# Branch B by halves of the queries, the third group's Q and K by residue, and merge sums on VectorE: one hybrid attention block on one core

## The chip, the cores and the metric

The kernel runs on 1 core of one Trainium2 chip. The metric is the device time of one execution in microseconds. Three runs of the kernel before are shown; its profile is one more execution.

## The reference

One decoder layer in float32, 2,048 tokens of width 1,024, batch 1. Token mixing: a normalised and modulated `h` goes through one input projection into two branches.

Branch A has 12 heads of 64 in three groups of 4, with (window, dilation) of (128, 1), (512, 4) and (2048, 16). A query at position t sees t, t-d, t-2d, ..., within the window, with a linear bias. The three groups' outputs are merged for each of 4 head slots with weights from their softmax denominators. Branch B has 4 heads of causal attention over all earlier tokens, with a forgetting bias:

```
qa, ka, va, qb, kb, vb, fz, gza, gzb = split(h @ w_in)
ya = dilated_mixture(qa, ka, va) @ w_up_a
yb = forgetting_attention(qb, kb, vb, fz, b_forget) @ w_up_b
x  = x + g1 * ((sigmoid(gza) * ya + sigmoid(gzb) * yb) @ w_out)
```

A gated feed-forward part and a last norm follow; the change doesn't touch them.

## The kernel before

All matrices are split into a high and a low part and multiplied in three products (`mm3`, L99) or, for scores, two. Stages in the order of the text: input projections, written to DRAM scratch; the two attention branches; the merge ("up"); the output projection; the feed-forward part. `build` (L1168) hands the whole trunk to a tile framework that places the instructions on the engines' queues from the order of the text and a planned timeline, allots buffers by tag and sets all waits. So the order of the text sets priorities and isn't kept to the letter.

Q and K (`qk_block`, L399). A projected block of 128 columns (two heads) by 512 tokens is evicted by `put` (L405) and stored to `qk_scr`. For the second group (dilation 4) the eviction reads the tokens with a stride of 4, so that the tokens of a residue lie side by side. The third group (dilation 16) is stored in token order.

Branch A (`branch_a`, L690). Each of the 12 heads loads its tiles with `head_tiles` (L657) and works in four steps u, each of four blocks of 128 queries. `scores` (L719) multiplies, adds the bias with a running maximum on VectorE (L735) and takes the exponential on ScalarE (L743); `sums` (L746) transposes the result on TensorE (L760), copies it (L767) and multiplies with the values (L771). The third group's score matmuls (L734) read queries and keys of residue bb straight from token order, `slice(bb, None, 16)`.

Branch B (`branch_b`, L887; `head_f`, L795). A head loads all its 2,048 queries and keys (high, low) and its values, four tiles of the tag "big", and goes through eight steps cq of two blocks of 128 queries each. A score segment of up to 512 keys takes a bias tile made on GpSimd (L813, L818; tag "t", 4 tiles), two matmuls (L825), a reduction on VectorE (L827) and an exponential on ScalarE (L837). `sums` (L841) transposes blocks of 128x128 (L861), splits them (L106 on ScalarE, L107 on VectorE) and multiplies with the values (L869). After each second cq the result goes to `u_scr` (L881).

Merge (`up(cp)`, L947, for the token half cp). Three groups' outputs of two head pairs are multiplied with merge weights and added (L964, L966, tiles of 128x1024, on GpSimd or VectorE by the tables UM and UA), branch B's two pairs are multiplied with their reciprocal denominators (L964); the results are split into y (L969). Then for each of 8 column blocks and 2 token chunks: 12 matmuls into two PSUM tiles, two products with the gates on VectorE (L989), one sum on GpSimd (L990), a store (L991). Per half: 8 products and 4 sums of 128x1024, 8 splits of y, 8 of weights, 192 matmuls, 32 gate products, 16 gate sums. y takes four "big" tiles.

Buffers: 11 tiles of the tag "big" (8 KiB a partition), 3 of "bigx", 6 of "mid", 6 each of "wh" and "wl" (branch B's score segments).

The order of work is set by `together` (L993): generators yield costs by hand, and the one whose clock, scaled by its pace, is lowest goes next. Branch A yields 2.0 for scores and 1.5 for sums of a step; branch B yields 0.7 (2cq + b + 1) / 4 for scores and 0.5 for each pair of key blocks in sums, and 0.5 at the end of a step; the merge yields 3.0 a step.

```
PACE = (0.6, 0.6)
ga, gb = branch_a(), branch_b()
together([(ga, PACE[0]), (gb, 1.0)])
merge_weights()
together([(gb, 1.0)], lambda: f_done[0] >= 4 * (NHB - 1) + 2)
gu = up(0)
together([(gu, PACE[1]), (gb, 1.0)])
for g in (gb, gu, up(1)): ...
```

`f_done` counts pairs of steps of branch B; 14 means that the last head has finished its first 1,024 queries. The loads of gates and weights in `up` stand behind the store `hold`, those of the output projection behind branch B's last store (`issue_after`).

Of the kernel before, what the change touches and what calls it, by code (L numbers as in the profile page):

```python
# [11 lines left out]
F32R = mybir.dt.float32r  # L12
# [6 lines left out]
P = 128  # L19
# [30 lines left out]
UT = (("pc",), ("wh", "wl"))  # L50
UM = ("GVGG", "GVGV")
UA = ("GG", "VV")

PACE = (0.6, 0.6)

# [4 lines left out]
def trunk(ctx, tc, x, c, w_ada, b_ada, norm_mix, w_in, b_forget, w_up_a, w_up_b, w_out,  # L60
# [338 lines left out]
    def qk_block(at_, hf, jL, jR):  # L399
        isq = jL < 6 or jL == 12  # L400
        sc = 0.125 if isq else 1.0
        col = lambda j: j * P if j < 12 else 2304 + (j - 12) * P
        a, b = 2 * hf, 2 * hf + 1

        def put(o, kept, j, ci):  # L405
            g = (j % 6) // 2 if j < 12 else 0
            d = DILS[g] if g < 2 else 1
            n = CH // d
            order = lambda ap: ap.rearrange("p (n r) -> p r n", r=d)
            place = lambda ap: ap.rearrange("p (r n) -> p r n", r=d)  # L410
            t = slot("s", "st")
            if kept is None:
                A.activation(place(t), order(o), AF.Copy, scale=sc)
            else:
                V.scalar_tensor_tensor(place(t), order(o), sc, order(kept), op0=ALU.mult, op1=ALU.add)
            hi = slot("t", "sh", dt=F32R)
            split(hi, t, t)
            for e in range(2):
                for i, part in enumerate((raw(hi), t) if isq else (raw(hi), t, raw(hi))):
                    SP.dma_start(place(qk_scr[j][e, i])[:, :, ci * n:(ci + 1) * n],  # L420
                                 place(part[64 * e:64 * e + 64, :]))
        t_block(at_, kcols(w_in, col(jL), P), kcols(w_in, col(jR), P),
                lambda o, t: put(o, t, jL, a), lambda o, t: put(o, t, jR, a),
                lambda o: put(o, None, jL, b), lambda o, t: put(o, t, jR, b), scale=sc)
# [230 lines left out]
    nev = [0]  # L655

    def head_tiles(qj, kj, half, vj, sl, d):  # L657

        r = []
        for n, j, part in (("qs", qj, 0), ("kh", kj, 0), ("kl", kj, 1)):  # L660
            r.append(slot("big", n, dt=F32R))
            SP.dma_start(raw(r[-1]), qk_scr[j][half, part:part + 2].rearrange("a p t -> (a p) t"))
        full = vj < 3
        if full:
            vhl = slot("mid", "va", [P, NT, 65])
            G.memset(vhl[:, :, 64:65], 1.0)
        else:
            vhl = slot("big", "vhl", [P, NT, P], F32R)
        src = v_scr[vj][:, sl, :]
        dst = vhl[:, :, :64] if full else raw(vhl)  # L670
        if d == 1:
            SP.dma_start(dst, src.rearrange("(n i) e -> i n e", i=P))
        else:
            src = src.rearrange("(n i r) e -> n i r e", r=d, i=P)
            dst = dst.rearrange("p (r n) e -> n p r e", r=d)
            for n in range(NT // d):
                SP.dma_start(dst[n], src[n])
        return (*r, vhl)

# [29 lines left out]
    def head_a(h):  # L709
# [9 lines left out]
        def scores(u):  # L719
# [4 lines left out]
            for b in range(4):  # L724
# [5 lines left out]
                o0 = P if first[b] else 0  # L730
                ksl = slice(bb, None, 16) if g == 2 else slice(k0, (bb + 1) * P)
                qsl = slice(bb, None, 16) if g == 2 else slice(bb * P, (bb + 1) * P)
                for i, kk in enumerate((kh, kl)):
                    PE.matmul(so[:, o0:], qs[:, qsl], kk[:, ksl], start=(i == 0), stop=(i == 1))  # L734
                V.tensor_tensor_reduce(out=Lb(b, o0, 256), in0=so[:, o0:], in1=bias[:, o0:],  # L735
# [58 lines left out]

    def head_f(h):  # L795
        qs, kh, kl, vhl = head_tiles(12 + h // 2, 14 + h // 2, h % 2, 3, h, 1)
        nf = [slot("mid", "nf") for _ in range(2)]
        for i in range(2):
            SP.dma_start(nf[i], brow(nf_scr[h, i * D:(i + 1) * D], D, P))
        uy, den, Ls = [None], {}, {}  # L800

        def scores(cq, b):
# [7 lines left out]
            for i, sg in enumerate(segs):  # L810
# [13 lines left out]
                for j, kk in enumerate((kh, kl)):  # L824
                    PE.matmul(s[:, :e - sg], qs[:, qb * P:(qb + 1) * P], kk[:, sg:e],  # L825
                              start=(j == 0), stop=(j == 1))
# [60 lines left out]
    def branch_b():  # L887

        behind = None
        for h in range(NHB):  # L890
            scores, sums = head_f(h)
            for cq in range(8):
                for b in range(2):
# [5 lines left out]
            if h == NHB - 1:  # L899
                yield from behind()  # L900
    f_end, f_done = [None], [0]

# [44 lines left out]
    def up(cp):  # L947
# [3 lines left out]
        for p_ in range(4):  # L951
            acc = None
            for g in range(3 if p_ < 2 else 1):
# [7 lines left out]
                for i in range(2):  # L961
                    SP.dma_start(wb[64 * i:64 * i + 64, :],
                                 bass.AP(tensor=src.tensor, offset=src.offset + i * T, ap=[[0, 64], [1, D]]))
                (V if UM[cp][g + (p_ > 1) * 3] == 'V' else G).tensor_tensor(uu, uu, wb, op=ALU.mult)  # L964
                if acc is not None:
                    (V if UA[cp][g - 1] == 'V' else G).tensor_tensor(uu, uu, acc, op=ALU.add)  # L966
                acc = uu
# [38 lines left out]
    merge_weights()  # L1006
    together([(gb, 1.0)], lambda: f_done[0] >= 4 * (NHB - 1) + 2)
    tt_only[0] = "U"
# [181 lines left out]
```

## Time and profile before

| | us |
|---|---|
| median of 3 runs (lowest, highest) | 2910.24 (2907.39, 2912.62) |
| the profiled execution, its time | 2907.55 |
| the profiled execution, its span from the first to the last instruction | 2905.8 |
| busy in the span: TensorE, VectorE, ScalarE, GpSimd | 2771.8, 2047.5, 1378.9, 217.4 |
| mean granted clock of TensorE, of full speed | 0.98 |

A matmul's row gives its start and a modelled end, and matmuls overlap. So a busy TensorE isn't one at its peak, and what a matmul costs is the distance between the starts of two that follow each other. The granted clock is 1 or 0.5 at any time; a window shows its mean.

### The profile page before, as it was taken

What the parts mean: (1) busy time and instruction counts of PE and PEld (TensorE: products, weight loads), DVE (VectorE), ACT (ScalarE), POOL (GpSimd) and SP (SyncE); (2) the same over time, 40 slices, a digit from 0 to 9 for tenths busy, and PEclk for the clock granted to TensorE, in tenths of its full rate; (3) what the DMA queues carried; (4) which work ended last, traced back from release to release, by engine and by line L of the source; (5) the groups of instructions that cost most, each with busy time, mean ns of one, the idle gap of its engine ahead of it and who ended that gap; (6) DMA issues with size and microseconds to landing.
All of it is one profiled execution on the core that took longest, in us unless ns stands there. A gap on an engine that the chain in (4) does not pass through costs nothing.

```text
span 2905.8 us, 40608 instructions
## 1 busy us (share of the span) xinstructions
PE 2771.8 (95%) x13666; PEld 2303.4 (79%) x13666; DVE 2047.5 (70%) x4281; ACT 1378.9 (47%) x2722; POOL 217.4 (7%) x305
## 2 busy tenths in 40 slices
PE   5899999999999999798899999999999999999998
PEld 3689888978888889676677788888888888878876
DVE  7765578576647887787877866657855558796887
ACT  4654345344447777663355633334433335343543
POOL 0000000000002222573300000000000000000000
PEclk8999999999999999899999999999999999999999
DMA  7587466467857656568856654344522235685642
GB/s 254 153 221 224 131 210 200 146 173 206 242 179 256 235 187 220 150 179 284 300 184 211 199 178 133 132 160 126 172 84 80 84 114 168 215 272 169 218 155 98
DMA packets 488409, 530.50 MB, mean 183 GB/s; under 512 B 58596, under 2 KB 339580, under 8 KB 481276
## 3 DMA queue, kind: packets, MB, share of 16 engines
q1 hardware_dynamic: 488200, 527.91, 57.4%
q8 instruction: 107, 1.75, 0.2%
q14 instruction: 102, 0.84, 0.1%
HBM read 356.51 MB, written 171.29 MB: 182 GB/s over the span
## 4 chain that ended last, share of the span: by engine, by line
PE 45%; DVE 3%; DMA 1%; issue 1%; ACT 1%; POOLq 0%; DVEq 0%; SPq 0%; ACTq 0%
PE psX L100 9%; PE psX L101 9%; PE psX L102 8%; PE psZ L100 4%; PE psZ L101 4%; PE psZ L102 4%; PE psY L101 2%; PE psY L100 2%; PE psY L102 2%; DMA x<-x 1%; DVE wl L107 1%; DVE wt L217 0%; PE psT L1065 0%; DMA out_dram<-x 0%; DVE x L1025 0%
## 5 line engine op out<-in xcount | busy, mean ns | idle before, releaser
L106 ACT ACTIVATE wh<-wt 128x512 fp32r<-128x512 f32 (+1 forms) x464 | 289.5, 626 | 639.9 <-PE psX L101 342.1
L107 DVE TENSOR_TENSOR wl<-wt,wh 128x512 fp32r<-128x512 f32 (+1 forms) x464 | 314.4, 681 | 260.6 <-ACT wh L106 240.7
L106 ACT ACTIVATE wh<-wr 128x512 fp32r<-128x512 f32 (+1 forms) x324 | 202.0, 624 | 447.5 <-PE psX L101 258.2
L107 DVE TENSOR_TENSOR wl<-wr,wh 128x512 fp32r<-128x512 f32 (+1 forms) x324 | 220.2, 680 | 192.6 <-ACT wh L106 171.1
L217 DVE TENSOR_TENSOR wt<-wr 128x512 f32<-128x512 f32 (+1 forms) x216 | 147.8, 684 | 12.5 <-DMA wr<-in_w_in_dram 6.6
L217 DVE TENSOR_TENSOR wt<-wr,wt 128x512 f32<-128x512 f32 (+1 forms) x216 | 147.0, 681 | 3.7
L244 ACT ACTIVATE u<-psX 128x512 f32<-128x512 f32 x216 | 125.7, 582 | 8.2 <-PE psX L102 8.2
L813 POOL TENSOR_SCALAR bi<-nf,F_col 128x512 f32<-128x512 f32 (+3 forms) x160 | 105.4, 660 | 247.8 <-DVE mx L827 206.4
L837 ACT ACTIVATE L<-L,nmf 128x512 f32<-128x512 f32 (+3 forms) x160 | 103.6, 650 | 19.7 <-DVE nmf L833 19.4
L1095 DVE TENSOR_TENSOR ac<-psZ,u 128x512 f32<-128x512 f32 x88 | 60.3, 687 | 42.2 <-PE psZ L102 41.2
L869 PE MATMUL psY<-ph,vhl 128*128 128x256 f32 (+1 forms) x288 | 83.9, 305 | 5.3 <-ACT ph L106 4.1
L106 ACT ACTIVATE ph<-psT 128x512 fp32r<-128x512 f32 (+1 forms) x101 | 57.1, 572 | 60.8 <-PE psT L861 60.0
L869 PE MATMUL psY<-pl,vhl 128*128 128x256 f32 (+1 forms) x288 | 82.5, 314 | 2.4 <-DVE pl L107 1.6
L735 DVE CUSTOM_DVE_ANT_0 L<-psX,bias 128x128 f32<-128x128 f32 (+1 forms) x192 | 64.7, 357 | 25.0 <-PE psX L734 22.3
L771 PE MATMUL psY<-pf,va 128*65 128x128 f32 (+1 forms) x408 | 78.5, 327 | 0.6 <-DVE pf L767 0.2
L107 DVE TENSOR_TENSOR pl<-psT,ph 128x512 fp32r<-128x512 f32 (+1 forms) x101 | 64.9, 646 | 20.0 <-ACT ph L106 19.6
L743 ACT ACTIVATE L<-L,nm 128x128 f32<-128x128 f32 (+1 forms) x192 | 72.6, 453 | 9.1 <-DVE nm L738 8.8
L100 PE MATMUL psZ<-y,wu 128*128 128x512 f32 x128 | 55.0, 429 | 16.3 <-DVE gt L989 14.5
L100 PE MATMUL psX<-f_A11h,wh 128*128 128x512 f32 x176 | 69.3, 394 | 0.0
L102 PE MATMUL psX<-f_A11h,wl 128*128 128x512 f32 x176 | 68.9, 392 | 0.0
L100 PE MATMUL psZ<-f_S4h,wh 128*128 128x512 f32 x176 | 68.7, 390 | 0.2 <-DVE ac L1095 0.2
L101 PE MATMUL psX<-f_A11l,wh 128*128 128x512 f32 x176 | 68.9, 392 | 0.0
(531 smaller groups left out, 8727.7 us busy)
## 6 DMA issues: line engine op xcount, KB each, us to landing
x<-x SPq DMA_DIRECT2D x192, 256.0 KB
wr<-in_w_ffn_in_dram SPq DMA_DIRECT2D x88, 512.0 KB
wr<-in_w_in_dram SPq DMA_DIRECT2D x64, 512.0 KB
qk<-sh SPq DMA_DIRECT2D x192, 128.0 KB
act<-ac SPq DMA_DIRECT2D x88, 256.0 KB
pc<-wfg SPq DMA_DIRECT2D x77, 256.0 KB
qk<-st SPq DMA_DIRECT2D x128, 128.0 KB
wa<-in_w_ada_dram SPq DMA_DIRECT2D x64, 256.0 KB
```

Of the source, the lines that this page charges most:

```text
L100: PE.matmul(o, lh, rh, start=first, stop=False, skip_group_check=True)
L101: PE.matmul(o, lh, rl, start=False, stop=False, skip_group_check=True)
L102: PE.matmul(o, ll, rh, start=False, stop=last, skip_group_check=True)
L106: A.activation(hi, src, AF.Copy)
L107: V.tensor_tensor(lo, src, raw(hi), op=ALU.subtract)
L217: V.tensor_tensor(v[i], *made[i](g, v), op=ALU.subtract)
L244: A.activation(t, o, AF.Copy, scale=1.0 if scale is None else scale)
L743: A.activation(Lb(b, o0, 256), Lb(b, o0, 256), AF.Exp, bias=nm[:, bb:bb + 1])
L771: PE.matmul(uo[:65, qb_[0] * P:qb_[0] * P + w], va[:, 4 * u + kb_, :], pf[:, pos:pos + w], start=i_ == 0, stop=i_ == len(runs) - 1, skip_g ...
L813: G.tensor_scalar(bi[:, :e - sg], nf[sg // D][:, sg % D:sg % D + e - sg], 1.0, F_col[:, qb * NHB + h:qb * NHB + h + 1], op0=ALU.mult, op1= ...
L837: A.activation(Ls[cq, b, sg][:, :e - sg], Ls[cq, b, sg][:, :e - sg], AF.Exp, bias=nm, accum_out=dp[:, i:i + 1])
L869: PE.matmul(uo[:, q0:256], vhl[:, kb, :], p_[:, 256 * i:256 * i + 256 - q0], start=(kp == 0 and i == 0 and j == 0), stop=(last and i == 1 ...
```

## The change

Four things. (1) The third group's Q and K are stored by residue within each chunk of 512 tokens; the queries are put in full residue order by four loads, the keys are read in four runs of 32 columns. (2) Branch B does the first 1,024 queries of all four heads and then the second 1,024 of all four. A first half loads half of the queries, keys and values, in two big tiles; a second half loads half of the queries and all keys and values, in four. (3) The first merged half starts once all first halves are done (`f_done` 8), beside the second halves; the paces are 0.45 and 1.5. (4) All merge products and sums of 128x1024 are on VectorE. The gate sums (L990) stay on GpSimd.

```diff
-UM = ("GVGG", "GVGV")
-UA = ("GG", "VV")
-PACE = (0.6, 0.6)
+PACE = (0.45, 1.5)
...
         def put(o, kept, j, ci):
             g = (j % 6) // 2 if j < 12 else 0
-            d = DILS[g] if g < 2 else 1
-            n = CH // d
+            d = DILS[g]
...
-                    SP.dma_start(place(qk_scr[j][e, i])[:, :, ci * n:(ci + 1) * n],
-                                 place(part[64 * e:64 * e + 64, :]))
+                    to, part = qk_scr[j][e, i], part[64 * e:64 * e + 64, :]
+                    if g == 1:
+                        SP.dma_start(place(to)[:, :, ci * CH // d:(ci + 1) * CH // d], place(part))
+                    else:
+                        SP.dma_start(to[:, ci * CH:(ci + 1) * CH], part)
...
+    def qk_rows(j, half, part):
+        return qk_scr[j][half, part:part + 2].rearrange("a p t -> (a p) t")
     def head_tiles(qj, kj, half, vj, sl, d):
...
+            to, src = raw(r[-1]), qk_rows(j, half, part)
+            if n == "qs" and d == 16:
+                for c_ in range(NCH):
+                    SP.dma_start(to.rearrange("p (r c n) -> p c r n", c=NCH, r=16)[:, c_],
+                                 src[:, c_ * CH:(c_ + 1) * CH].rearrange("p (r n) -> p r n", r=16))
+            else:
+                SP.dma_start(to, src)
...
+    def half_tiles(h, part):
+        qj, kj, half, n = 12 + h // 2, 14 + h // 2, h % 2, (part + 1) * D
+        if part == 0:
+            t = [slot("big", "kk", dt=F32R), slot("big", "qv", dt=F32R)]
+            kh, kl = [t[0][:, i * D:(i + 1) * D] for i in range(2)]
+            qs, vhl = t[1][:, :D], t[1][:, D:].rearrange("p (n e) -> p n e", e=P)
+        else:
+            kh, kl, qs, vhl = [slot("big", nm, dt=F32R) for nm in ("kh", "kl", "qs", "vhl")]
+            qs, vhl = qs[:, :D], vhl.rearrange("p (n e) -> p n e", e=P)
+        SP.dma_start(raw(qs), qk_rows(qj, half, 0)[:, n - D:n])
+        for i, kk in enumerate((kh, kl)):
+            SP.dma_start(raw(kk), qk_rows(kj, half, i)[:, :n])
+        SP.dma_start(raw(vhl), v_scr[3][:n, h, :].rearrange("(n i) e -> i n e", i=P))
+        return qs, kh, kl, vhl
...
-                ksl = slice(bb, None, 16) if g == 2 else slice(k0, (bb + 1) * P)
-                qsl = slice(bb, None, 16) if g == 2 else slice(bb * P, (bb + 1) * P)
                 for i, kk in enumerate((kh, kl)):
-                    PE.matmul(so[:, o0:], qs[:, qsl], kk[:, ksl], start=(i == 0), stop=(i == 1))
+                    if g == 2:
+                        PE.matmul(so[:, o0:].rearrange("p (c n) -> p c n", c=NCH), qs[:, bb * P:(bb + 1) * P],
+                                  kk.rearrange("p (c r n) -> p r c n", c=NCH, r=16)[:, bb],
+                                  start=(i == 0), stop=(i == 1))
+                    else:
+                        PE.matmul(so[:, o0:], qs[:, bb * P:(bb + 1) * P], kk[:, k0:(bb + 1) * P],
+                                  start=(i == 0), stop=(i == 1))
...
-    def head_f(h):
-        qs, kh, kl, vhl = head_tiles(12 + h // 2, 14 + h // 2, h % 2, 3, h, 1)
-        nf = [slot("mid", "nf") for _ in range(2)]
-        for i in range(2):
+    def head_f(h, part):
+        qs, kh, kl, vhl = half_tiles(h, part)
+        nf = [slot("mid", "nf") for _ in range(part + 1)]
+        for i in range(part + 1):
...
-        for h in range(NHB):
-            scores, sums = head_f(h)
-            for cq in range(8):
+        for part, h in [(p_, h) for p_ in range(2) for h in range(NHB)]:
+            scores, sums = head_f(h, part)
+            for cq in range(4 * part, 4 * part + 4):
...
-                (V if UM[cp][g + (p_ > 1) * 3] == 'V' else G).tensor_tensor(uu, uu, wb, op=ALU.mult)
+                V.tensor_tensor(uu, uu, wb, op=ALU.mult)
                 if acc is not None:
-                    (V if UA[cp][g - 1] == 'V' else G).tensor_tensor(uu, uu, acc, op=ALU.add)
+                    V.tensor_tensor(uu, uu, acc, op=ALU.add)
...
-    together([(gb, 1.0)], lambda: f_done[0] >= 4 * (NHB - 1) + 2)
+    together([(gb, 1.0)], lambda: f_done[0] >= 2 * NHB)
```

## Rows read from the trace of the kernel before

**Rows 1.** The page's first part: busy us (share of the span) xinstructions.
```profile
PE 2771.8 (95%) x13666; PEld 2303.4 (79%) x13666; DVE 2047.5 (70%) x4281; ACT 1378.9 (47%) x2722; POOL 217.4 (7%) x305
```

**Rows 2.** Windows, the four stretches around the attention branches; the first line names the columns.
```profile
core 0: us, PE busy (x) PEld busy (x) DVE busy (x) ACT busy (x) POOL busy (x), PEclk, DMA share, GB/s
885.00:1188.00 303.00, 292.70 (x1977) 257.34 (x1977) 241.42 (x934) 230.88 (x552) 81.63 (x163) 0.98 0.64 215
1188.00:1268.00 80.00, 62.19 (x351) 50.46 (x349) 59.49 (x174) 48.53 (x122) 50.60 (x59) 0.85 0.39 107
1268.00:1353.00 85.00, 75.11 (x397) 62.80 (x396) 68.20 (x134) 39.75 (x92) 45.73 (x39) 0.92 0.90 269
1353.00:1440.00 87.00, 69.67 (x278) 51.51 (x277) 69.82 (x98) 24.51 (x43) 31.94 (x20) 0.96 0.92 318
```

**Rows 3.** Windows of line L861 alone (branch B's transposes): PE busy (x), PEld busy (x).
```profile
885.00:1188.00 303.00, 50.94 (x316) 38.48 (x316) 0.98 0.64 215
1188.00:1268.00 80.00, 24.05 (x129) 17.43 (x129) 0.85 0.39 107
1268.00:1353.00 85.00, 16.86 (x99) 12.47 (x99) 0.92 0.90 269
```

**Rows 4.** Timeline of PE near 1099 us, third group's scores: start us, us, instruction.
```profile
1099.31 0.39 PE L734 MATMUL psX<-kl,qs 128*128 128x128 f32 x1
1099.53 0.39 PE L734 MATMUL psX<-kh,qs 128*128 128x128 f32 x1
```

**Rows 5.** Timeline of PE near 1278 us, branch B's scores.
```profile
1277.83 0.39 PE L825 MATMUL psX<-kl,qs 128*128 128x512 f32 x1
1278.06 0.22 PE L825 MATMUL psX<-kh,qs 128*128 128x128 f32 x1
1278.11 0.28 PE L825 MATMUL psX<-kl,qs 128*128 128x128 f32 x1
1278.23 0.33 PE L869 MATMUL psY<-ph,vhl 128*128 128x256 f32 x1
```

**Rows 6.** Windows, parts of the first stretch; columns as in rows 2.
```profile
900.00:1095.00 195.00, 189.26 (x1314) 162.22 (x1313) 163.46 (x607) 145.25 (x349) 50.94 (x101) 1.00 0.59 200
1095.00:1140.00 45.00, 42.79 (x262) 40.11 (x260) 29.81 (x125) 32.11 (x76) 9.63 (x21) 0.89 0.77 254
```

**Rows 7.** Line L415, evictions of Q and K: ns min/median/max, first and last start.
```profile
L415 DVE SCALAR_TENSOR_TENSOR st<-psZ,u x32: 682/691/1083, 99.1 to 747.9; 128x512 f32<-128x512 f32 x32
```

**Rows 8.** DMA queue, 1102 to 1108 us (packets, MB, share), and SP's timeline there.
```profile
q1 hardware_dynamic: 3094, 0.76, 63.5%
...
1102.50 3.06 SPq L677 DMA_DIRECT2D va<-v  x2
```

**Rows 9.** Windows, 885 to 1440 us: sums of line L827, then of tile pl.
```profile
sum 555.00, DVE 102.48; mean DVE 25.62
...
sum 555.00, PE 82.45 PEld 58.33 DVE 91.81; mean PE 20.61 PEld 14.58 DVE 22.95
```

**Rows 10.** Line L964, merge products on VectorE: ns min/median/max.
```profile
L964 DVE TENSOR_TENSOR uw<-uw x6: 1224/1566/2262, 1212.7 to 1366.3; 128x1024 f32<-128x1024 f32 x6
```

**Rows 11.** Windows of tile y: PE, PEld, DVE, ACT busy (x); the DVE part is its splits.
```profile
1188.00:1268.00 80.00, 0.68 (x3) 0.60 (x4) 5.31 (x6) 3.57 (x6) 0.85 0.39 107
```

**Rows 12.** Groups of POOL, 1188 to 1353 us: busy, mean ns, idle before and releasers.
```profile
L813 POOL TENSOR_SCALAR bi<-nf,F_col 128x512 f32<-128x512 f32 (+3 forms) x52 | 37.5, 726 | 29.8 <-DVE mx L827 25.1 <-DVE den L839 3.6 <-DVE nmf L833 1.1
L964 POOL TENSOR_TENSOR uw<-uw 128x1024 f32<-128x1024 f32 x10 | 24.1, 2414 | 16.6 <-DMA uw<-wrow 9.2 <-ACT L L837 4.3 <-DMA uw<-u 2.5
...
L966 POOL TENSOR_TENSOR uw<-uw 128x1024 f32<-128x1024 f32 x4 | 9.5, 2374 | 0.0
```

**Rows 13.** Line L989, gate products on VectorE.
```profile
L989 DVE TENSOR_TENSOR gt<-psZ,gt x64: 658/680/694, 1271.2 to 1434.2; 128x512 f32<-128x512 f32 x64
```

**Rows 14.** Window 1260 to 1280 us; columns as in rows 2.
```profile
1260.00:1280.00 20.00, 19.66 (x126) 16.90 (x126) 18.30 (x57) 14.79 (x41) 11.05 (x17) 1.00 0.59 170
```

**Rows 15.** Line L990, gate sums: what ended POOL's idle time before them (us, times).
```profile
  DVE gt L989: 55.0, 21
```

More of the change, by code (lines that the diff above doesn't have):

```diff
@@ L661, in head_tiles @@
             r.append(slot("big", n, dt=F32R))
[L662 to L670, printed above, removed]
+            to, src = raw(r[-1]), qk_rows(j, half, part)
[5 more added lines that the diff above has]
+                SP.dma_start(to, src)
+        va = slot("mid", "va", [P, NT, 65])
+        G.memset(va[:, :, 64:65], 1.0)
+        src, dst = v_scr[vj][:, sl, :], va[:, :, :64]
         if d == 1:
@@ L677, in head_tiles @@
                 SP.dma_start(dst[n], src[n])
-        return (*r, vhl)
+        return (*r, va)
+    def half_tiles(h, part):
[12 more added lines that the diff above has]
+        return qs, kh, kl, vhl
     base = cst.tile([P, 256], F32, name="base")
@@ L824, in scores @@
                 for j, kk in enumerate((kh, kl)):
-                    PE.matmul(s[:, :e - sg], qs[:, qb * P:(qb + 1) * P], kk[:, sg:e],
+                    PE.matmul(s[:, :e - sg], qs[:, (qb % 8) * P:(qb % 8 + 1) * P], kk[:, sg:e],
                               start=(j == 0), stop=(j == 1))
@@ L900, in branch_b @@
                 yield from behind()
+                behind = None
     f_end, f_done = [None], [0]
```

## The prediction

> **What bounds the kernel now.** I read the page first: TensorE is busy 95% of the span [rows 1]. A share over 2.9 ms hides stages, so I cut the stretch that the change touches at four events: both attention branches start (885 us), branch A ends (1188), the first merged products run (1268), branch B ends (1353), the output projection begins (1440). Those windows [rows 2] show different limits. In the first, 303 us, TensorE is busy 97% and VectorE 80%: TensorE is the bound. In the second, 80 us, branch B is alone: TensorE 62 of 80 us at a granted clock of 0.85, VectorE 59. In the third branch B runs beside the merged halves, VectorE 68 of 85. In the fourth the merged halves run beside the preparation of the output projection: DMA share 0.92, VectorE 70 of 87. Idle TensorE time, the thing to win, is 10, 18, 10 and 17 us. Branch B's progress is counted by its transposes of 128x128 score blocks: 316, 129 and 99 in the first three windows, 544 in all [rows 3].
>
> The sum is made against the profiled execution, 2907.55 us (span 2905.8); the median of the three runs stands 2.7 us above it, within their scatter, so the forecast serves for both. What a measurement of this kernel can tell from no change is about 0.2%, 6 us.
>
> **Part 1: how much of branch B runs beside branch A.** Branch A's generator yields 12 x 4 x 2.0 + 48 x 1.5 = 168 units. At pace 0.6 branch B gets 100.8 units meanwhile, at 0.45 it gets 75.6. A first half of a head costs 6.3 + 5 = 11.3 units (36 blocks), a second half 17.5 + 13 = 30.5 (100 blocks). So 75.6 units are all four first halves and one second half: 144 + 100 = 244 blocks, where 316 ran before. 72 blocks leave the first window. Price of a block on TensorE: 62.19 us x 0.85 / 129 = 0.41 us [rows 2, 3]. That takes 29.5 us from the first window; it isn't a gain, since the blocks come back later.
>
> **Part 2: residue order for the third group.** Before, its scores read queries and keys with a stride of 16 elements. Successive matmuls of 128 columns start 0.22 us apart, so a pair (high and low part) takes 0.44 us [rows 4]. With contiguous operands such a pair takes 0.17 us: starts at 1278.06, 1278.11, 1278.23 [rows 5]. There are 4 heads x 16 pairs: 64 x 0.27 = 17 us. The new moving operand is four runs of 32 columns, which no row shows: at worst it costs as much as before (0 gained), at best the full 17. I take 16, as the runs are nearer to contiguous than to a stride of 16, and as the weights (queries) become fully contiguous. In 1095 to 1140, where this group starts, the granted clock is 0.89 although TensorE is busy 43 of 45 us [rows 6]: 0.11 x 45 = 5 us lost. I count it as regained, lower end 0.
> The price: 12 evictions on VectorE (three of four per pair, two pairs, two token halves) read with a stride. The evictions of the second group do that already and are the slow ones of this line, 1.08 us at most against a median of 0.69 [rows 7]: 12 x 0.39 = 4.7 us, in projection stages where TensorE is the bound; taken as 0, at worst 4.7. The queries of these heads now load by 4 x 4 transfers of 2,048 pieces of 128 B. The nearest row has pieces of 256 B: 3,094 packets took 63.5% of 6 us on 16 DMA engines, 20 ns each, and SP was busy 3.06 us with two issues [rows 8]. So 32,768 pieces cost at most 40 us of DMA time over 255 us, 0.16 on a share of 0.64, and SP some 6 us a head ahead of branch B's loads. Both are covered by loading one head ahead; if that cover fails, some 5 us a head, 20 us.
>
> **Part 3: first window after.** 292.7 - 29.5 - 16 - 5 = 242 us of TensorE, plus the 10 us idle: 252 (bounds 252 and 273). VectorE gives up 72 x 0.375 = 27 of its 241 us, and 214 of 252 is 85%, what 900 to 1095 sustains (163 of 195) [rows 6]. The block price on VectorE: at least (102.48 + 91.81) / 544 = 0.357 us for scores and splits alone [rows 9]; at most (59.49 - 5.31 - 2 x 1.57) / 129 = 0.396 in the window of branch B [rows 2, 10, 11]; I take the middle.
>
> **Part 4: second half of branch B beside the first merged half.** The condition f_done >= 8 is met when branch A ends, so nothing waits: 300 blocks and up(0) run together (91.5 units against 60 x 1.5 = 90, so they end together). The window of branch B alone goes, and with it the queue on GpSimd: 14 products and sums of 2.4 us stood in one queue with 52 biases of 0.73 us there [rows 12], and branch B's scores wait on those biases. TensorE: 300 x 0.41 + 192 x 0.23 = 167 us (a matmul of 512 columns is followed after 0.23 us [rows 5]). VectorE: blocks 300 x 0.375 = 112; 32 gate products at 0.68 = 22 [rows 13]; 22 splits of y and weights at 5.31 / 6 = 0.89 = 20 [rows 11]; 22 of the 24 merge products and sums, which were 14 on GpSimd and 10 on VectorE. One takes 1.22 us at the least and 2.26 at the most [rows 10]; the median is 1.57 while GpSimd works over half of the time, it will work less, so 1.45: 32 us. Sum 186 us, so VectorE is the bound. At the 0.915 that it reached where branch B ran beside the merged half without GpSimd products (18.30 of 20 us, TensorE 19.66) [rows 14] the stretch takes 204 us; bounds 186 (always busy) and 233 (0.80, as in the third window before).
> Branch B loads 22 MB instead of 16 (keys and values of the first half twice) and 12 bias rows instead of 8; over 250 and 204 us that keeps DMA near 0.65: 0. A second-half head holds 4 of 11 big tiles and y 4 more, so the next head's values wait for a tile; the sums need them a step later: 0, at worst 5 us for each of 2 changes.
>
> **Part 5: tail.** At branch B's end 39 of 64 gate products and the preparation of the output projection were left; after, 32 are left, the same preparation, and y's last quarter, which needs the last head. Its loads start behind branch B's last store as now. DMA sets it: 85 instead of 87 us, bounds 80 and 95.
>
> **Sum.** Before 303 + 80 + 85 + 87 = 555. After 252 + 204 + 85 = 541, 14 us less: 2907.6 - 14 = **2894 us**. With every bound at its worse end it is 273 + 233 + 95 = 601, at its better end 252 + 186 + 80 = 518; the ends hardly come together, so the range below is cut by the cases.
>
> **Rivals.**
> *TensorE stays the bound, a larger gain.* If VectorE keeps up, the middle stretch takes 167 / 0.96 = 174 us, as dense as the first window: 252 + 174 + 85 = 511, so 2864. For: 18.30 of 20 with TensorE at 19.66. Against: the sum gives VectorE more work than TensorE.
> *GpSimd's queue, slower.* The 16 gate sums of up(0) stay on GpSimd, in one queue with the biases of 300 blocks. Such a sum sat waiting for VectorE's gate product 55 us in 21 waits, 2.6 us each [rows 15]. A bias behind it holds branch B's scores. 16 x 2.6 = 42 us on top of 204: 2894 + 42 = 2936. It decides only once a wait outlasts the cover of the four bias tiles, some four segments of 0.75 us and their waits, about 3 to 9 us; the mean wait is below that, so I give it little. A partial case, half of the waits, is 2915.
> *The shared interface.* The ten products that VectorE already did took up to 2.26 us beside GpSimd, 1.22 alone [rows 10]. If all 22 run beside the biases at 2.26: 22 x 0.81 = 18 us more on the bound, / 0.915 = 20: 2914. If they meet as often as before, 1.57, 3 us more: 2897. The Trainium skill, GPSIMD Engine Reference, Specifications, says that GpSimd shares its SBUF interfaces with VectorE and contends with its instructions that have two SBUF inputs. By that rule these products slow GpSimd's biases too; this trace agrees as far as VectorE's own spread goes.
> *The moving reads gain nothing.* Four short runs as slow as the stride: first window 268 to 273, so 2910 to 2915, no change to slightly slower.
>
> **Chances.** Forecast 0.44 (of it 0.36 faster by over 6 us, 0.08 within); larger gain 0.27; GpSimd's queue 0.13, slower; shared interface 0.09 (0.03 faster, 0.03 same, 0.03 slower); reads gain nothing 0.07 (0.01, 0.02, 0.04). Faster 0.67, same 0.13, slower 0.20. The range leaves out the far end of the larger gain and the full queue case: 2858 to 2920.
>
> **What would show it.** Right: third-group score matmuls start near 0.06 and 0.11 us apart; branch A ends near 1137 us; the first merged matmul comes some 45 us later, not 80; branch B and up(0) end near 1341 us with VectorE over 88% busy; the granted clock stays at 1 in between. Wrong: biases waiting behind gate sums and TensorE's score loads waiting for VectorE (queue); merge products at 2 us (interface); score starts still 0.2 us apart (reads); the output projection starting after 1440.

## The result and the profile after

The changed kernel is slower by 0.6%: 2925.13 us (median of 5 runs, 2921.73 to 2932.03) against 2907.39 us for the kernel before on the same chip (5 runs, 2900.47 to 2912.62). The ratio is 1.0064, interval [1.0041, 1.0087]. The forecast was 2894, with a range up to 2920.

Busy time from the page of the changed kernel, which answers to [rows 1]: TensorE has 10.5 us less work, GpSimd 33 us less, VectorE 12 us more, and the span is 17.6 us longer.

```profile
span 2923.4 us, 40639 instructions
...
PE 2761.3 (94%) x13666; PEld 2286.0 (78%) x13666; DVE 2059.2 (70%) x4295; ACT 1378.0 (47%) x2722; POOL 184.3 (6%) x291
```

Windows of the changed kernel, cut at the same events as [rows 2]: both branches start, branch A ends, branch B ends, and the point 11 us later than before where the output projection stands as far as it did at 1440 (its first matmuls start at 1426.8 instead of 1417.3, its 252nd at 1508.1 instead of 1496.3).

```profile
core 0: us, PE busy (x) PEld busy (x) DVE busy (x) ACT busy (x) POOL busy (x), PEclk, DMA share, GB/s
885.00:1158.00 273.00, 253.82 (x1772) 216.64 (x1771) 211.97 (x866) 205.82 (x489) 66.60 (x139) 0.99 0.77 236
1158.00:1375.00 217.00, 179.13 (x1007) 144.29 (x1005) 177.04 (x402) 119.00 (x284) 81.01 (x110) 0.96 0.71 212
1375.00:1451.00 76.00, 56.86 (x225) 43.61 (x224) 60.28 (x89) 23.55 (x41) 26.26 (x16) 0.87 0.91 306
```

Branch B's transposes alone (L887 of the changed kernel, as [rows 3]) show 234 blocks in the first window and 311 in the second:

```profile
885.00:1158.00 273.00, 36.51 (x234) 27.71 (x235) 0.99 0.77 236
1158.00:1375.00 217.00, 50.69 (x311) 37.27 (x310) 0.96 0.71 212
```

Read against before, the first window is 30 us shorter (303 to 273), with 82 blocks fewer. The stretch from branch A's end to branch B's is 52 us longer (165 to 217), with those blocks and more of the merged half in it. The last stretch is 11 us shorter (87 to 76). Sum 566 against 555. The other 6 us lie behind the 252nd projection matmul, in a part that the change doesn't touch: 1415.3 us here, 1409.5 before. The profiled executions of the kernels below spread there from 1409 to 1416 us, and nothing was tried on it.

The profile pointed to two things. First, VectorE isn't full in the middle stretch: 177 of 217 us, 0.82. Its waits there are led by the merge products, which wait for their row of weights, and TensorE's by VectorE:

```profile
DVE uw L992 <- DMA uw<-wrow: 10.8, 11, 2.1
DVE wu L105 <- ACT wu L104: 5.7, 3, 3.5
...
PE psX L851 <- DVE mx L853: 15.8, 17, 3.2
PE psY L895 <- DVE pl L105: 10.7, 14, 1.6
```

(Columns: us in total, times, longest.) Second, the third group's reads did get faster. Its score matmuls, which started 0.22 us apart [rows 4], start here 0.11 to 0.16 us apart:

```profile
1120.98 0.33 PE L755 MATMUL psX<-kh,qs 128*128 128x128 f32 x1 [0.36 <-DVE mxa L761]
1121.14 0.27 PE L755 MATMUL psX<-kl,qs 128*128 128x128 f32 x1
1121.26 0.28 PE L755 MATMUL psX<-kh,qs 128*128 128x128 f32 x1
1121.37 0.28 PE L755 MATMUL psX<-kl,qs 128*128 128x128 f32 x1
```

But the loads that put the queries in order hold SP's queue for 7 to 10 us a head. This is SP's timeline in the changed kernel (start, us, line, transfer): one head's four query loads (L669), and behind them the values, the results, the denominators and the statistics of another head:

```profile
1070.75 10.00 SPq L669 DMA_DIRECT2D qs<-qk  x4
1080.85 2.89 SPq L682 DMA_DIRECT2D va<-v  x1
1083.83 1.44 SPq L812 DMA_DIRECT2D u<-utok  x1
1085.32 0.43 SPq L813 DMA_DIRECT2D den<-utok  x1
1085.85 0.33 SPq L818 DMA_DIRECT2D sta<-str  x1
1089.02 0.34 SPq L939 DMA_DIRECT2D md<-den  x1
1089.52 0.32 SPq L946 DMA_DIRECT2D md<-sta  x1
```

The merge weights read those statistics, and VectorE stood 5.1 us on them, with TensorE behind it (waits between 1085 and 1100):

```profile
DVE mw L960 <- DMA md<-sta: 5.1, 1, 5.1
...
PE psX L755 <- DVE mxa L761: 4.9, 1, 4.9
```

### The profile page after: what moved, and what is told of

Read it like the earlier page. It is cut to its first block, busy times and chain, and to the rows that moved or that the text cites. A ratio compares the mean times of both kernels' runs of the same rounds, so it can differ in the third digit from the quotient of the medians.

```text
span 2923.4 us, 40639 instructions
## 1 busy us (share of the span) xinstructions
PE 2761.3 (94%) x13666; PEld 2286.0 (78%) x13666; DVE 2059.2 (70%) x4295; ACT 1378.0 (47%) x2722; POOL 184.3 (6%) x291
## 4 chain that ended last, share of the span: by engine, by line
PE 48%; DMA 5%; DVE 4%; issue 1%; ACT 1%; SPq 0%; POOLq 0%; POOL 0%; DVEq 0%; ACTq 0%
PE psX L98 9%; PE psX L99 9%; PE psX L100 9%; PE psZ L98 5%; PE psZ L99 5%; PE psZ L100 5%; PE psY L99 2%; PE psY L98 2%; PE psY L100 2%; DMA uw<-wrow 1%; DMA wr<-in_w_up_b_dram 1%; PE psY L895 1%; DMA kl<-qk 0%; PE psX L851 0%; DMA h2sp<-pe 0%
## 5 line engine op out<-in xcount | busy, mean ns | idle before, releaser
L839 POOL TENSOR_SCALAR bi<-nf,F_col 128x512 f32<-128x512 f32 (+3 forms) x160 | 106.4, 667 | 260.3 <-DVE mx L853 210.5
L104 ACT ACTIVATE ph<-psT 128x512 fp32r<-128x512 f32 (+1 forms) x126 | 71.3, 573 | 69.4 <-PE psT L887 67.4
L105 DVE TENSOR_TENSOR pl<-psT,ph 128x512 fp32r<-128x512 f32 (+1 forms) x126 | 81.5, 653 | 9.8 <-ACT ph L104 9.4
L769 ACT ACTIVATE L<-L,nm 128x128 f32<-128x128 f32 (+1 forms) x192 | 72.5, 450 | 18.9 <-DVE nm L764 17.6
L887 PE MATMUL psT<-ident,L 128*128 128x128 f32 x477 | 77.0, 281 | 1.4 <-ACT L L863 1.1
L895 PE MATMUL psY<-pl,vhl 128*128 128x256 f32 x208 | 60.0, 315 | 12.8 <-DVE pl L105 10.9
L98 PE MATMUL psZ<-y,wu 128*128 128x512 f32 x128 | 54.2, 425 | 17.6 <-ACT y L104 10.6
```

The source lines that it names most:

```text
L98: PE.matmul(o, lh, rh, start=first, stop=False, skip_group_check=True)
L104: A.activation(hi, src, AF.Copy)
L105: V.tensor_tensor(lo, src, raw(hi), op=ALU.subtract)
L839: G.tensor_scalar(bi[:, :e - sg], nf[sg // D][:, sg % D:sg % D + e - sg], 1.0, F_col[:, qb * NHB + h:qb * NHB + h + 1], op0=ALU.mult, op1= ...
L887: PE.transpose(pt[:, n:n + P], Ls[cq, b, sg][:, kb * P - sg:kb * P - sg + P], ident)
L895: PE.matmul(uo[:, q0:256], vhl[:, kb, :], p_[:, 256 * i:256 * i + 256 - q0], start=(kp == 0 and i == 0 and j == 0), stop=(last and i == 1 ...
```

## The experiments

Thirteen kernels, each timed 4 to 11 times. The kernel before was timed beside every group of them (medians 2905.28 to 2907.28), and the ratio is against that.

| run | median us | ratio to before, interval |
|---|---|---|
| e1_residue_alone | 2910.10 | 1.0006 [0.9997, 1.0015] |
| e2_without_residue | 2927.02 | 1.0068 [1.0056, 1.0081] |
| e3_queries_stored_by_residue | 2921.62 | 1.0052 [1.0038, 1.0066] |
| e4_merge_on_both | 2920.12 | 1.0046 [1.0034, 1.0059] |
| e5_pace_a_06 | 2940.49 | 1.0115 [1.0100, 1.0131] |
| e6_merge_pace_25 | 2936.82 | 1.0109 [1.0094, 1.0125] |
| e7_second_half_loads_late | 2925.79 | 1.0066 [1.0053, 1.0078] |
| e8_banks_shared | 2962.34 | 1.0187 [1.0173, 1.0201] |
| e9_halves_alone | 2912.28 | 1.0018 [1.0009, 1.0027] |
| e11_before_pace_045 | 2925.64 | 1.0061 [1.0048, 1.0074] |
| e1r_residue_stored_alone | 2899.10 | 0.9972 [0.9961, 0.9983] |
| e12_merge_late | 2932.26 | 1.0097 [1.0081, 1.0112] |
| e13_residue_stored_pace_072 | 2917.25 | 1.0047 [1.0033, 1.0061] |

**e1 and e2: the residue order alone, and all but it.** e1 is the kernel before with part (1) of the diff; e2 the changed kernel with the third group as before.

> The kernel before with the residue order of the third group alone (its stores, its loads in small pieces, its score matmuls in four runs). Theory S (SP's queue): the reads gain 64 x 0.18 = 12 us of TensorE, but the small-piece loads hold SP for 10 us a head and VectorE stalls behind a late load, so the gain is given back: between -4 and +6 us against before (2903 to 2913). Rival R (the loads are covered): the 12 us stay, about 2895. In both, score matmuls of the third group start 0.11 to 0.14 us apart instead of 0.22.

> The changed kernel without the residue order: third group stored in token order and read with a stride of 16, one load of queries a head. Theory S: the SP queue is free again and the stride costs its 12 us, so within 5 us of the changed kernel (2920 to 2930), with no stall of VectorE behind the merge weights' load near 1086 us. Rival R: 10 to 12 us slower than the changed kernel (2936). If it is faster than the changed kernel by over 6 us, the residue order is a net loss.

Neither way does the residue order, with its loads, gain anything in the whole time: e1 is within 0.15% of before, and e2's interval lies inside that of the changed kernel. So most of the loss is not in this part, and neither is any gain.

**e3: queries in order by the stores.** The changed kernel, with the third group's queries stored in full residue order while the projections run, and one load a head:

```diff
-                    if g == 1:
+                    if g == 1 or g == 2 and isq:
...
-            if n == "qs" and d == 16:
...
+            SP.dma_start(to, src)
```

> The changed kernel, but the third group's queries are put in full residue order when they are stored (runs of 32 tokens to DRAM, in the projection stage), and each head loads them with one transfer of 8 KiB rows. Theory S: SP is free beside branch A, the reads' gain stays; branch A ends near 1140 us instead of 1158, and the time is 10 to 18 us below the changed kernel (2907 to 2915). Rival: the first window was long because of branch A's own chain; then branch A ends at 1155 to 1160 and the time is within 4 us of the changed kernel.

The median is 3.5 us below the changed kernel and the intervals overlap, so by its time this is a miss for theory S, and what its rival had asked for. Branch A ends between the two, at 1151.3 us. Its end in e2, in the changed kernel and in e3 (last start of its value matmuls) gives the size of both effects:

```profile
L787 PE MATMUL psY<-pf,va x408: 270/377/477, 893.7 to 1158.5; 128*65 128x128 f32 x72, 128*65 128x256 f32 x64
...
L797 PE MATMUL psY<-pf,va x408: 271/324/432, 894.4 to 1157.8; 128*65 128x128 f32 x72, 128*65 128x256 f32 x64
...
L791 PE MATMUL psY<-pf,va x408: 271/295/477, 893.9 to 1151.3; 128*65 128x128 f32 x72, 128*65 128x256 f32 x64
```

With the stride branch A ends at 1158.5; with the faster reads and their loads at 1157.8; with the reads and without the loads at 1151.3. The reads are worth some 7 us of the first window, and the loads take them. e1r below shows the like in the kernel before.

**e4: merge sums on both engines.** The changed kernel with the tables of before.

```diff
+UM = ("GVGG", "GVGV")
+UA = ("GG", "VV")
...
-                V.tensor_tensor(uu, uu, wb, op=ALU.mult)
+                (V if UM[cp][g + (p_ > 1) * 3] == 'V' else G).tensor_tensor(uu, uu, wb, op=ALU.mult)
```

> The changed kernel with the merge products and sums divided between GpSimd and VectorE as before (14 and 10). Theory V (VectorE bounds the stretch of branch B beside the merge): 15 us less on VectorE, so 8 to 15 us faster than the changed kernel (2910 to 2917). Rival G (GpSimd's queue): the 2.4 us products stand before branch B's biases again, 5 to 20 us slower than the changed kernel. Rival L (latency of the chain sets the stretch, not VectorE's work): within 4 us.

5 us below the changed kernel by the medians, between theory V and rival L; the intervals overlap, so it is not clear of noise. The wait for the row of weights moves along with the products: in the same stretch VectorE's is 5.1 us instead of 10.8, and GpSimd has 10.5.

```profile
DVE uw L994 <- DMA uw<-wrow: 5.1, 3, 3.4
...
POOL uw L994 <- DMA uw<-wrow: 10.5, 7, 3.2
```

**e5: the old pace.** The changed kernel with one number put back.

```diff
-PACE = (0.45, 1.5)
+PACE = (0.6, 1.5)
```

> The changed kernel with branch A's pace put back to 0.6 (merge pace 1.5): some 83 more of branch B's blocks run beside branch A. Theory B (a block is cheap beside branch A, 0.36 us, and dear beside the merge, 0.70 us, where branch B's own chain sets the pace): branch A ends near 1188, branch B near 1345, and the time falls by 15 to 28 us to 2897 to 2910. Rival T (a block costs the same wherever it runs, since TensorE or VectorE is full in both): branch A ends 30 us later, branch B where it did, time within 5 us of the changed kernel.

15 us slower than the changed kernel. 314 blocks ran beside branch A again, but soon after branch A's end TensorE stood 19 us for the next second half's keys. Their loads are in SP's queue behind loads of the merged half (L984), which wait for tiles that VectorE's sums hold. Waits of e5, 1189 to 1258 us for TensorE and 1150 to 1240 for SP, and then SP's timeline:

```profile
PE psX L851 <- DMA kh<-qk: 19.3, 1, 19.3
...
SPq L984 <- DVE uw L994: 14.0, 4, 6.5
```

```profile
1215.04 0.33 SPq L984 DMA_DIRECT2D uw<-u  x1
1215.41 1.08 SPq L990 DMA_DIRECT2D uw<-wrow  x2
1216.59 0.53 SPq L696 DMA_DIRECT2D qs<-qk  x1
1217.22 0.38 SPq L698 DMA_DIRECT2D kh<-qk  x1
```

By its numbers the theory of cheap blocks beside branch A fell here; but a new wait stood in its way, so the pace was not tested by itself. e11 does that.

**e6, e7, e8: three misses.** The changed kernel with less of the merged half beside branch B; with the second merged half's loads held until the first has stored five of its eight column blocks; with branch B using the merged half's PSUM banks too.

```diff
-PACE = (0.45, 1.5)
+PACE = (0.45, 2.5)
...
+                    if cp:
+                        late.enter_context(tc.issue_after(m_hold[0]))
...
-SCT = {"A": "X", "F": "Z", "E": "XZ", "U": "X"}
-PTT = {"A": "T", "F": "TTZ", "E": "TTZ", "U": "T"}
+SCT = {"A": "X", "F": "Z", "E": "XZ", "U": "XZ"}
+PTT = {"A": "T", "F": "TTZ", "E": "TTZ", "U": "TTZ"}
```

> The changed kernel with the merge's pace 2.5 in place of 1.5: some 40% of the first merged half is left when branch B ends and can cover the last head's way through store, load, product and split. Theory C (no cover at branch B's end costs the 10.6 us gap): branch B ends 5 to 15 us earlier, the gap is gone, 5 to 12 us faster than the changed kernel (2913 to 2920). Rival: the merge's work is only moved behind branch B, within 4 us of the changed kernel. Theory B alone (the chain sets branch B's pace whatever runs beside it): branch B ends at 1370 or later all the same.

> The changed kernel with the loads of the second merged half's products held behind a store of the first half's fifth column block: 12 MB of loads and 11 products leave 1200 to 1290 us. Theory D (the stretch is long because DMA is full from 1180 to 1280 us and branch B's next head loads late): DMA share falls below 0.9 there, branch B ends 8 to 15 us earlier, the time is 5 to 12 us below the changed kernel. Rival: within 4 us or slower, since the second half's products come later.

> The changed kernel with branch B drawing its score and transpose banks from X, Z and T, T, Z also beside the merge (as it does alone), not from X and T alone. Theory P (two banks for scores and two for transposes make branch B's chain slow beside the merge): branch B ends 10 us or more earlier and the time falls by 5 to 15 us. Rival: the merge's matmuls wait for Z in turn, no change or up to 15 us slower.

e6 is 12 us slower: branch B ends no earlier with less merged work beside it (last value matmul at 1376.8 against 1374.7, in the slowest of its four executions), so the merged half filled gaps there. e7 changes nothing in the time, though the DMA share from 1180 to 1280 us falls from 0.96 to 0.77: the loads of the second merged half aren't what holds this stretch. e8 is 37 us slower. Its longest wait, 21.2 us, is that of a merged matmul for a split of y on ScalarE; how the shared banks lead to it was not shown (waits of TensorE, 1160 to 1410 us):

```profile
PE psZ L98 <- ACT y L104: 24.1, 3, 21.2
```

**e9 and e11: order and pace, one at a time.** e9 is the kernel before with branch B by halves and the half tiles alone, merged half at `f_done` 14. e11 is the kernel before with one number changed. e9, then e11:

```diff
+        for part, h in [(p_, h) for p_ in range(2) for h in range(NHB)]:
+            scores, sums = head_f(h, part)
...
-PACE = (0.6, 0.6)
+PACE = (0.45, 0.6)
```

> Of the change only the order of branch B by halves is kept, with its half tiles. The third group's queries and keys, the shares of VectorE and GpSimd in the merge sums, the pace beside branch A (0.6) and the point where the first merged half starts (100 blocks of 128x128 left) are those of the kernel before. Theory O, the order by halves is itself dearer (keys and values loaded twice, second halves of 9 to 16 blocks a row one behind the other): 10 to 20 us slower than before, branch B's end at 1365 to 1375 us instead of 1353. Theory E, the early start of the merged half beside 300 blocks is what costs: within 4 us of before, branch A's end near 1188 and branch B's near 1353. Theory R, a block is cheap while it fills TensorE's gaps beside branch A and dear afterwards, so the lower pace is what costs: within 4 us of before as well, since some 315 blocks still run beside branch A; the next run tells E and R apart.

> The kernel before with one number changed: branch B's pace beside branch A is 0.45 instead of 0.6, so some 235 blocks instead of 316 run beside branch A and some 80 more run after it. Order, merge sums and merged start stay. Theory R (those 80 blocks give branch A back 30 us and cost 45 to 50 us later): 12 to 20 us slower than before, branch A's end near 1158 and branch B's near 1368. Theories E and O (a block costs the same 0.4 us of TensorE on either side): within 5 us of before, since the 30 us that branch A gains are paid back one for one.

This is the largest cost found. In the kernel before, the pace alone costs 18.5 us by the medians, as much as the whole change. The order alone costs 5 us, half of what theory O asked for and a little over what E and R allowed. Windows of e11 from the start to its branch A's end (1156) and to branch B's end (1364), and then its transposes alone:

```profile
885.00:1156.00 271.00, 260.38 (x1749) 226.56 (x1749) 210.38 (x822) 199.17 (x472) 60.89 (x122) 0.99 0.68 234
1156.00:1364.00 208.00, 171.71 (x958) 141.08 (x956) 158.46 (x418) 117.48 (x291) 114.18 (x137) 0.90 0.54 155
```

```profile
885.00:1156.00 271.00, 36.42 (x238) 28.27 (x238) 0.99 0.68 234
1156.00:1364.00 208.00, 55.75 (x306) 39.96 (x306) 0.90 0.54 155
```

78 blocks left the first window and shortened it by 32 us (303 to 271): 0.41 us each, the price of the prediction. They came back in the second stretch, which grew by 43 us (165 to 208): 0.55 us each. In the first window branch B's blocks stand between branch A's and TensorE is busy 96% at a clock of 0.99. After it TensorE is busy 0.83 of the time at a clock of 0.90, as it was before from 1188 to 1353 us (0.83, clocks of 0.85 and 0.92 [rows 2]), so the same work takes longer there. Of the 0.55 us, some 0.44 is TensorE's busy time for a block (0.41 in the first window); the rest is idle time. TensorE's longest waits there are for branch B's own reductions and splits on VectorE (waits of e11, 1156 to 1364 us):

```profile
PE psX L825 <- DVE mx L827: 9.2, 6, 4.9
PE psY L869 <- DVE pl L107: 7.4, 8, 4.1
```

Some 4 us more come in the tail: the merged matmuls end 15 us later than before, at 1445.0 instead of 1430.0.

That the pace costs as much inside the changed kernel is not shown, as e5 met a new wait. e12 below and e9 both do branch B by halves and start the merge late; they differ in the paces, the merge products and the residue order, and e12 stands 22 us further above the kernel before than e9 does. If products and residue order take some 8 of these, 14 are left for the paces: an estimate, of the same order as e11's 18.5.

**e1r: the residue order without the loads.** The kernel before with part (1), and the queries stored in order as in e3.

> The kernel before with the residue order for the third group alone, but with the queries stored in full residue order by the stores of the projection stage (pieces of 128 bytes there) and loaded in one transfer a head; the keys as in the change. Theory S (the four-part loads of 2,048 pieces hold the queue of SP for 10 us a head and eat the gain of the faster reads): branch A's end 7 to 10 us earlier than before, 3 to 8 us faster in all. Rival (what the faster reads win beside branch A is lost after it, whatever the loads do): within 3 us of before.

8 us faster than before, and faster than both kernels: theory S holds. Branch A's last value matmul starts at 1179.6 instead of 1188.2, and a head's query load takes SP 0.3 to 0.7 us instead of 7 to 10 (group of that line in e1r; last starts of the value matmuls of A and B):

```profile
L665 SPq DMA_DIRECT2D qs<-qk x8: 319/341/737, 1004.4 to 1141.5; - x8
...
L778 PE MATMUL psY<-pf,va x408: 271/324/479, 895.1 to 1179.6; 128*65 128x128 f32 x72, 128*65 128x256 f32 x64
...
L876 PE MATMUL psY<-pl,vhl x288: 272/282/579, 894.3 to 1341.9; 128*128 128x256 f32 x144
```

**e12 and e13: does the early merged half pay, and does the pace help upwards?** e12 is the changed kernel with the merged half started late again; e13 is e1r at a higher pace.

```diff
-    together([(gb, 1.0)], lambda: f_done[0] >= 2 * NHB)
+    together([(gb, 1.0)], lambda: f_done[0] >= 4 * (NHB - 1) + 2)
...
-PACE = (0.6, 0.6)
+PACE = (0.72, 0.6)
```

> The changed kernel with one condition put back: the first merged half starts when 100 blocks of branch B are left, as before, instead of at branch A's end with some 300 left. Theory G (the lower pace costs 18 us, and the early merged half pays about 10 of it back by filling TensorE beside branch B): 6 to 12 us slower than the changed kernel, near 2933. Rival N (the early start fills nothing, since VectorE bounds that stretch either way): within 3 us of the changed kernel, near 2925. Rival H (the early start costs): faster than the changed kernel by 4 us or more.

> The kernel before with the third group in residue order, queries stored in that order, and branch B's pace beside branch A raised from 0.6 to 0.72, so some 380 blocks run beside branch A instead of 316. Theory R (a block costs 0.41 us of the stretch beside branch A and 0.55 us after it): branch A's end some 25 us later, at 1205, and the whole 4 to 9 us faster than the same kernel at pace 0.6, so 2890 to 2895. Rival (at 0.6 the gaps beside branch A are used up, further blocks cost as much there as after): within 3 us of 2899.

e12 is 7 us slower than the changed kernel by the medians, 10 by the ratios; the intervals overlap slightly. Theory G fits best: the early merged half pays part of the pace's cost back. e13 is a miss, 18 us slower than e1r. Its 60 further blocks (379 against e1r's 319) made branch A's window 35.5 us longer, 0.59 us each: at 0.6 the cheap gaps are used up. Branch B ends only 6 us later, and the other 12 us come behind it: more of the merged half is left then, and its matmuls wait for splits of the up weights (last start of branch A's value matmuls in e13, then one of the two largest of TensorE's waits from 1150 to 1400 us):

```profile
L778 PE MATMUL psY<-pf,va x408: 270/273/691, 896.6 to 1215.1; 128*65 128x128 f32 x72, 128*65 128x256 f32 x64
```

```profile
PE psZ L100 <- ACT wu L106: 11.6, 4, 5.0
```

## Why the prediction was wrong

By its own terms: the first window was to be 252 us and is 273; the middle 204 and is 217; the tail 85 and is 76; the sum 541 and is 566. With the 6 us behind it that is the 31 us between 2894 and 2925.

Two steps failed. Part 2's gain of 21 us in the first window did not come, for two reasons given below. And part 4 took the stretch behind branch A for as dense as its densest 20 us, so that a block costs 0.41 us there as it does in the first window; e11 shows 0.55. The first alone would have left a smaller gain; the second is why the change loses time.

**Part 1** was right: 234 blocks instead of 244 stayed, and e11 shows that a block is worth 0.41 us of the first window. Its sentence "it isn't a gain, since the blocks come back later" was right too. But part 4 lets them come back at 0.375 us of VectorE, at a share of 0.915, which is 0.41 us again. Taking blocks out of the first window was a loss of its own, 18.5 us in e11, and the prediction had no such case among its rivals.

**Part 2** was too high, and then failed at "Both are covered by loading one head ahead". The pair of matmuls takes some 0.25 us, not the 0.44 of before and not the 0.17 hoped for: 64 x 0.19 = 12 us, where 16 were taken, and 5 us of clock on top. With the loads out of the way branch A ends only 7 to 9 us earlier (e3 against e2, e1r against before), not 21. The clock did not come back with the reads: in e1r it is still 0.89 from 1095 to 1140 us, and over the first window it is 0.99 in the changed kernel as in e2 and e11, which keep the stride. Of the 7 us the loads leave 1 (e2 against the changed kernel). The transfers themselves were priced; what was not is what stands behind them in SP's queue, at 7 to 10 us a head where the prediction said "some 6". The worst case it named for a failed cover, 20 us, is near the 21 us that the first window lacks, but by luck: 14 of these are a gain that wasn't there, and the loads took some 7. In the kernel before they cost 11 us in all (e1 against e1r, by the medians), part of it behind branch A.

**Part 4** made VectorE's work the bound. VectorE wasn't full, though its reductions and splits lead TensorE's waits (15.8 and 10.7 us). The price of the work was slightly high: a merge product took 1.23 us as the median of 15 and 1.33 as their mean, where 1.45 was taken. Its work in the stretch was 177 us, where the sum had 186. Two views of these products in the middle stretch, by tile (ns min/median/max) and by group (busy us, mean ns, idle before and releasers):

```profile
L992 DVE TENSOR_TENSOR uw<-uw x15: 1207/1226/2206, 1181.4 to 1287.2; 128x1024 f32<-128x1024 f32 x15
```

```profile
L992 DVE TENSOR_TENSOR uw<-uw 128x1024 f32<-128x1024 f32 x15 | 19.9, 1329 | 15.1 <-DMA uw<-wrow 10.8 <-DMA uw<-rc 3.7 <-issue 0.5
```

It failed at "At the 0.915 that it reached": that share was that of one 20 us window [rows 14], and over the stretch it was 0.82. In the second window before it had been 0.74 and in the third 0.80 [rows 2]. 177 us at 0.915 would have been 193: the other 24 us are this share alone. TensorE's share there is 0.83, the same as before from 1188 to 1353 us and in e11, and not the 0.96 of the first window. Products that came to VectorE brought their wait for the weights row along (15.1 us idle before them), and the queue behind them holds the reductions and splits that TensorE waits for; e4 puts some 5 us on it, not clear of noise. 311 blocks instead of 300 add an estimated 6 us at 0.55. What the rest of the low share comes from stays open: e6, e7 and e8 each tried a cause, and none made the stretch shorter.

**Part 5** was too high by 9 us. 30 gate products were left where 32 were expected, but DMA, which was to set this part, moved less: some 23 MB (76 us at 306 GB/s) where before it moved 28 (87 at 318 [rows 2]).

**The rivals.** *GpSimd's queue* fell: GpSimd idled 21.5 us before the 16 gate sums of this stretch, 1.3 us each instead of 2.6, and no bias came late for it. In the whole execution VectorE, which reads the biases, waited twice for them, 0.3 us each, and both times beside branch A (one of the two, line L839, who waited for it: us, times):

```profile
  DVE L L853: 0.3, 1
```

*The shared interface* exists but met few products. Of the 23 products and sums of 128x1024 on VectorE in this stretch, 13 ran while GpSimd ran nothing: 1.20 to 1.23 us each. The other 10 took 1.21 to 2.21 us, and the longest, 2.21 and 1.72, ran beside gate sums:

```profile
1235.80 2.54 POOL L1018 TENSOR_TENSOR gt<-gt 128x512 f32<-128x512 f32 x2 [2.48 <-DVE gt L1017]
1237.22 2.21 DVE L992 TENSOR_TENSOR uw<-uw 128x1024 f32<-128x1024 f32 x1 [0.30 <-DMA uw<-wrow]
```

In all that is some 2.3 us over 23 x 1.22, where the rival had 18. The Trainium skill, GPSIMD Engine Reference, Specifications, has GpSimd contend with two-input VectorE instructions; this trace agrees: alone no product took over 1.23 us, and beside GpSimd's work seven of the ten took 1.30 to 2.21. In time no rival came near: *reads gain nothing* and the partial case of GpSimd's queue end at 2915, 10 us below what was measured, the full queue 11 us above, and the runs bear out none of their reasons; the reads did gain.

**The parts do not add up exactly.** By medians, the first three against before and the last two against the changed kernel: pace 18.5, halves 5, residue order 3, merge products 5, early merged half -7: 24.5, where 18 were measured. By the intervals the halves and the residue order are known to some 3 us, the last two to some 8.

## What to carry to other kernels

A stretch that is dense because two streams fill each other's gaps is worth more than its time per block: price work that leaves it at what it costs where it lands, not at what it frees. Count a reordering load in issue time on its queue, and name everything behind it; in the kernel before, the same reordering, put into the stores of an earlier stage, let the gain through (e1r). Moving work to another engine moves its waits there too.

## What the runs showed of the hardware that was not expected

With the moving operand in four runs of 32 columns and contiguous weights, matmuls of 128 columns start 0.11 to 0.16 us apart; with a stride of 16 elements in both it was 0.22 [rows 4]. The weight loads got shorter with it (0.19 us each here at 1121 us, 0.31 before at 1099), so how much of the gain belongs to the moving operand isn't shown. Four transfers of 2,048 pieces of 128 B held SP's queue for 10.0 us in the head shown and for 6.7 to 10.3 us in the four heads, single ones for 0.4 to 6.2 us; one transfer of the same tile in whole rows holds it for 0.3 to 0.7 us (e1r). A product of 128x1024 on VectorE took 1.20 to 1.23 us while GpSimd ran nothing, and up to 2.21 us beside a gate sum on GpSimd.
